# Two additions of an MLP convolution moved from VectorE to adding transfers on GpSimd's queue

## The chip, the cores and the metric

The kernel runs on one core of a Trainium2 chip. The core has a matrix engine (TensorE, PE in the profile; its weight loads are PEld), a vector engine (VectorE, DVE), an activation engine (ScalarE, ACT), a general engine (GpSimd, POOL) and a queue engine (SyncE, SP). Each works through its own instructions in order and waits on semaphores for the others. Transfers are issued from a queue of one of the engines and carried out by 16 DMA engines. The metric is the device time of one execution in microseconds, as a median of several.

## What is computed

An encoder trunk of two layers over 256 tokens of 1024 channels, in fp32. The first half of a layer is a token mixer (pooling and attention branches). The second half, which the change is about, is a gated MLP with a depthwise convolution of width 3 along the tokens:

```python
def _conv_ffn(xn, w_up, conv_w, conv_b, w_down):
    a, gval = jnp.split(xn @ w_up, 2, axis=-1)
    a = lax.conv_general_dilated(a, conv_w[:, None, :], window_strides=(1,),
                                 padding=((CONV_WIDTH // 2, CONV_WIDTH // 2),),
                                 dimension_numbers=('NWC', 'WIO', 'NWC'),
                                 feature_group_count=D_FF) + conv_b
    return (jax.nn.gelu(a) * gval) @ w_down
```

D_FF is 2816, that is 22 chunks of 128 channels. Token t of a channel needs the products of its own value, of the value before and of the value after, each with its own weight, and their sum.

## The kernel before

**Weight pieces.** TensorE multiplies numbers that are split into a high part in a shortened format and a rest, in three products (high by high, high by rest, rest by high). Every weight matrix is loaded from HBM in tiles `raw` (three buffers, loads on SP, L163), and each half of a tile, a *piece* of 128 x 1024, is split by a cast on ScalarE (`wh`, L242) and a subtraction on VectorE (`wl`, L244). There are five buffers for split pieces. `W.get()` takes the next piece for TensorE and splits the pieces ahead; in the stretches with an order written out by hand it opens the piece four ahead, whose buffer is that of the piece just used up. `open_next` returns the two steps of a split, and `run_between` puts waiting VectorE steps between them.

**Places.** The MLP is a row of *places*, one for each piece, with 12 matmuls of 512 columns each. `MLP_GROUPS` (L43) lists groups of four places: "a" are columns of the convolved branch, "g" of the gate branch, "b" the last two chunks of both, and "d" are rows of w_down: the product of the results with w_down accumulates in four PSUM banks. The group that is entered first has places 4 to 7; the loop at L1471 counts places from 8 on.

**Crossings.** An "a" or "g" group gives rows of tokens. At the first place of the next group, `cross` (L737) turns them on VectorE in blocks, writes 512 KB to DRAM from SP, and some places later SP reads them back with channels on the partitions (`zga`, `zg`, `zb`).

**Pairs.** The 22 chunks are taken in 11 pairs. For a pair, `steps_up(f)` gives five steps:

- `fetch_up` (ScalarE, L1397): from the crossed branch, for each of the two chunks, the product for the token before (`a0`), the middle one with bias (`y`), and that for the token after (`a2`), brought into the order of the tokens;
- `neighbours` (VectorE, L1409): two additions, of `a0` into `y` shifted by one token, and of `a2` into `y` shifted the other way;
- `activate` (ScalarE, L1414): the Gelu, in place on `y`;
- `gate` (VectorE, L1417): times the gate branch;
- `keep_up` (L1424): the split of the product into two parts, as TensorE needs it (copy on ScalarE, subtraction on VectorE).

`PAIR_PLACES` (L48) gives for each pair (p1, p3). Steps in `between` of a place run on VectorE between the cast and the rest of the piece opened there; steps in `behind` come behind the place's work, sorted by rank. Before the change: fetch behind p1, neighbours between at p1 + 1, activate behind p1 + 1, gate between at p3 and keep_up behind p3. Each list is in the engine's own order, so an engine that waits in one step holds everything behind it.

**The end of the MLP.** `residual_mm` (L615) multiplies with w_down. The last four rows of chunks (18 to 21) are held back and used together. When no pair step is left, the order by hand ends and the last pieces are run with the order that the scheduler makes (L1487 to L1493). The first layer goes over into the next layer's norm and value products, the second into the last norm and the stores.

Of the kernel before, what the change touches and what calls it, by code (L numbers as in the profile page):

```python
# [13 lines left out]
ALU = mybir.AluOpType  # L14
# [4 lines left out]
S = 256  # L19
# [21 lines left out]


MLP_GROUPS = (  # L43
    ("g", 0), ("a", 1), ("g", 1), ("d", 0), ("a", 2), ("g", 2), ("a", 3), ("g", 3), ("b", 20),
    ("a", 4), ("g", 4), ("d", 4), ("d", 8), ("d", 12), ("d", 16), ("d", 20),
)

PAIR_PLACES = (  # L48
    (11, 14), (14, 16), (19, 22), (23, 26), (31, 34), (35, 38), (40, 42), (44, 46), (51, 54), (56, 58), (53, 56),
)  # L50
HALVES = (slice(0, 512), slice(512, D))
SEGMENTS = (HALVES, (slice(0, 512), slice(512, 768), slice(768, D)))

# [226 lines left out]
def encoder(ctx, tc, x, w_in, w_pool, pool_scale, w_a, w_b, w_o, norm1, norm2, w_up, conv_w,  # L280
            conv_b, w_down, rel_bias, norm_f, onehot, edges, out):
    nc = tc.nc
# [28 lines left out]
    for l in range(DEPTH):  # L311
# [8 lines left out]
        for kind, n in GROUPS:  # L320
            c0 = {"u": 0, "q": C_Q, "k": C_K}[kind] + n * 512
            pieces = rows(w_in[l], 0, 4, c0, 512)
            if (kind, n) in POOLS:
                g, at = POOLS[kind, n]
# [445 lines left out]
    def begin_values_of_x():  # L770
# [32 lines left out]
        def square(t, n):  # L803
            cc = HALVES[n]
            junk = sm.tile([P, 512], F32, tag="p", bufs=3, name="junk")
            nc.scalar.activation(
                junk, h[:, t, cc], AF.Square, scale=D**-0.5, accum_out=ss[t][:, n : n + 1]
            )
            if n == 0:
                nc.gpsimd.tensor_scalar_add(ss[t][:, 3:4], ss[t][:, 0:1], EPS)  # L810
            else:
                nc.gpsimd.tensor_add(out=ss[t][:, 3:4], in0=ss[t][:, 3:4], in1=ss[t][:, 1:2])
                return nc.gpsimd.tensor_tensor(out=rs[t], in0=ss[t][:, 3:4], in1=mhalf, op=ALU.pow)
# [146 lines left out]
    for l in range(DEPTH):  # L960
# [274 lines left out]
        def keep_gated(n):  # L1235
# [4 lines left out]
            for t in range(2):  # L1240
                nc.vector.scalar_tensor_tensor(
                    out=gated["pa"][:, t, HALVES[n]], in0=th[t], scalar=1.0, in1=ps[t],
                    op0=ALU.add, op1=ALU.mult,
# [28 lines left out]
        with tc.manual_schedule():  # L1272
# [27 lines left out]
            first = None  # L1300
            for n, cc in enumerate(HALVES):
                ps = None
# [10 lines left out]
                y = big.tile([P, 2, 4, 4, 32], F32, tag=("q0", "k0")[n], name="turned")  # L1313
                z = big.tile([P, 2, 4, 4, 32], F32, tag=("q1", "v0")[n], name="merged")
                first = []
                for t in range(2):
                    nc.vector.scalar_tensor_tensor(
                        out=th[:, t], in0=th[:, t], scalar=1.0, in1=ps[t], op0=ALU.add, op1=ALU.mult
# [52 lines left out]
        def branch(kind, f, count=1):  # L1371

            n, c = divmod(f, 4)
            z, c = (z_of[kind, n], c) if n < NQ else (z_of["b", 4 * NQ], c + 2 * (kind == "g"))
            return z[:, :, c : c + count].rearrange("p (t a) c j -> p c t a j", t=2)
# [13 lines left out]
        def steps_up(f):  # L1389

            t = {}

            def row(j, c):
                k = j * NF + f + c
                return prm[:, l, k : k + 1]

            def fetch_up():  # L1397
                for name, tag in (("a0", "u"), ("y", "s"), ("a2", "us")):
                    t[name] = sm.tile([P, 2, S], F32, tag=tag, name=name)
                for c in range(2):  # L1400
                    a = branch("a", f + c)[:, 0]
                    for j, name in enumerate(("a0", "y", "a2")):
                        out = t[name][:, c].rearrange("p (a j t) -> p t a j", t=2, j=32)
                        if j == 1:
                            nc.scalar.activation(out, a, AF.Identity, bias=row(3, c), scale=row(1, c))
                        else:
                            nc.scalar.mul(out=out, in_=a, mul=row(j, c))  # L1407

            def neighbours():  # L1409
                y = t["y"]  # L1410
                nc.vector.tensor_add(out=y[:, :, 1:], in0=y[:, :, 1:], in1=t["a0"][:, :, : S - 1])
                nc.vector.tensor_add(out=y[:, :, : S - 1], in0=y[:, :, : S - 1], in1=t["a2"][:, :, 1:])

            def activate():  # L1414
                nc.scalar.activation(t["y"], t["y"], AF.Gelu_apprx_tanh)

            def gate():  # L1417
                g = t["g"] = sm.tile([P, 2, 2, P], F32, tag="p", bufs=3, name="g")
                nc.vector.tensor_mul(
                    out=g.rearrange("p c t (a j) -> p c t a j", j=32),  # L1420
                    in0=t["y"].rearrange("p c (a j t) -> p c t a j", t=2, j=32), in1=branch("g", f, 2),
                )

            def keep_up():  # L1424
                n = f % NH
                ah, al = (x[n >= HPG][:, n - HPG * (n >= HPG) :][:, 0:2] for x in (acth, actl))
                nc.scalar.copy(out=ah, in_=t["g"])
                nc.vector.tensor_sub(out=al, in0=t["g"], in1=ah.bitcast(F32))
                for c in range(2):
                    acts[f + c] = (ah[:, c], al[:, c])  # L1430

            return fetch_up, neighbours, activate, gate, keep_up

        between, behind = {}, {}
        for f, (p1, p3) in zip(range(0, NF, 2), PAIR_PLACES):
            fetch_up, neighbours, activate, gate, keep_up = steps_up(f)
            for at, p, rank, step in (
                (behind, p1, 2, fetch_up), (between, p1 + 1, 1, neighbours), (behind, p1 + 1, 1, activate),
                (between, p3, 0, gate), (behind, p3, 0, keep_up),
            ):  # L1440
                at.setdefault(p, []).append((rank, f, step))
# [82 lines left out]
```

## Time and profile before

| | us |
|---|---|
| median of 3 runs | 855.04 (854.87 to 856.85) |
| the profiled execution | 854.74 |
| its span, first to last instruction | 853.0 |
| TensorE busy in the span | 846.1 |
| VectorE busy | 606.0 |
| ScalarE busy | 501.1 |
| GpSimd busy | 34.8 |

The mean granted TensorE clock is 0.998. HBM gives 186.02 MB and takes 27.28 MB. The busy time is a sum over the span; the time that an engine did not work shows who waited only together with the waits. A matmul is recorded until its result has left the pipe, so one after the other they overlap. The MLP of the first layer lies at about 250 to 427 us of the span, that of the second at about 670 to 850.

### The profile page before, as it was taken

Reading aid. Unit: us, or ns where it says so; the run is one execution under the profiler, and the core shown is the slowest. Engines: PE = TensorE matmul, PEld = TensorE weight load, DVE = VectorE, ACT = ScalarE, POOL = GpSimd, SP = SyncE. Lnnn points to the kernel's source line nnn. Section 1 sums busy time; section 2 is a strip of 40 time slices with the busy share of each in tenths; the row PEclk is TensorE's granted clock in tenths of the full one; section 3 lists DMA queues with packets and bytes.
Section 4 is the critical chain, followed back from the end, with each engine's and each line's share of the span. In section 5 each row is a group of like instructions: output and inputs, shape, how many; then the busy total and the mean of one; then the engine's idle time right before and its main releaser. Section 6 shows DMA issues by size and latency. Waiting matters only on the chain.

```text
span 853.0 us, 10910 instructions
## 1 busy us (share of the span) xinstructions
PE 846.1 (99%) x3925; PEld 706.7 (83%) x3925; DVE 606.0 (71%) x794; ACT 501.1 (59%) x727; POOL 34.8 (4%) x96
## 2 busy tenths in 40 slices
PE   9999999999999999999999999999999999999997
PEld 7888888888888888888888888888888888888886
DVE  6958877767766776777755687868577767777674
ACT  7744566654543775758545454577454557566682
POOL 1710000000010000000000000000000100000000
PEclk9999999999999999999999999999999999999999
DMA  8698897796747979997726899768777489898931
GB/s 302 213 304 284 302 287 251 250 295 212 249 179 281 280 258 299 285 297 223 243 102 214 261 281 324 252 224 262 244 261 267 145 288 303 248 287 291 296 141 50
DMA packets 147966, 214.03 MB, mean 251 GB/s; under 512 B 7800, under 2 KB 69184, under 8 KB 147912
## 3 DMA queue, kind: packets, MB, share of 16 engines
q1 hardware_dynamic: 147480, 212.67, 76.6%
q8 instruction: 31, 0.51, 0.2%
q10 hardware_dynamic: 432, 0.66, 0.2%
q14 instruction: 23, 0.19, 0.1%
HBM read 186.02 MB, written 27.28 MB: 250 GB/s over the span
## 4 chain that ended last, share of the span: by engine, by line
PE 98%; DVE 1%; ACT 0%; POOL 0%; issue 0%; DVEq 0%; ACTq 0%; POOLq 0%
PE t_ps L694 64%; PE v_ps L694 6%; PE res_ps L611 6%; PE res_ps L612 6%; PE res_ps L613 6%; PE v_ps L940 3%; PE v_ps L839 1%; PE pool_ps L598 1%; PE o_ps L1223 1%; PE s_ps L1175 1%; PE s_ps L1170 1%; PE o_ps L1219 1%; PE xt_ps L525 1%; PE warm_ps L400 0%; PE xt_ps L790 0%; DVE h L505 0%
## 5 line engine op out<-in xcount | busy, mean ns | idle before, releaser
L244 DVE TENSOR_TENSOR wl<-raw,wh 128x1024 fp32r<-128x1024 f32 x274 | 331.7, 1220 | 157.5 <-ACT wh L242 156.4
L694 PE MATMUL t_ps<-wh,x 128*128 128x512 f32 x1408 | 439.2, 390 | 0.0
L242 ACT CAST wh<-raw 128x1024 fp32r<-128x1024 f32 x274 | 285.0, 1049 | 200.6 <-PE t_ps L694 132.0
L694 PEld LDWEIGHTS t_ps<-wh,x 128*128 128x128 f32 x1408 | 264.3, 188 | 55.0
L694 PE MATMUL t_ps<-wl,x 128*128 128x512 f32 x704 | 273.9, 389 | 0.0
L694 PEld LDWEIGHTS t_ps<-wl,x 128*128 128x128 f32 x704 | 132.2, 188 | 27.2
L613 PE MATMUL res_ps<-wh,actk 128*128 128x512 f32 (+1 forms) x184 | 69.8, 380 | 0.0
L611 PE MATMUL res_ps<-wh,actq 128*128 128x512 f32 (+1 forms) x184 | 69.8, 380 | 0.0
L612 PE MATMUL res_ps<-wl,actq 128*128 128x512 f32 (+1 forms) x184 | 69.7, 380 | 0.0
L694 PE MATMUL t_ps<-wh,po 128*128 128x512 f32 x128 | 41.4, 395 | 0.0
L612 PEld LDWEIGHTS res_ps<-wl,actq 128*128 128x128 f32 x184 | 34.6, 188 | 6.7
L613 PEld LDWEIGHTS res_ps<-wh,actk 128*128 128x128 f32 x184 | 34.6, 188 | 6.6
L611 PEld LDWEIGHTS res_ps<-wh,actq 128*128 128x128 f32 x184 | 34.6, 188 | 6.5
L1407 ACT ACTIVATE a<-zga,prm 128x256 f32<-128x256 f32 x80 | 39.0, 514 | 0.0
L490 POOL TENSOR_SCALAR ss<-ss 128x1 f32<-128x1 f32 x8 | 2.1, 266 | 771.9 <-ACT junk L483 771.9
L694 PEld LDWEIGHTS t_ps<-wh,po 128*128 128x128 f32 x128 | 24.1, 188 | 4.9
L611 PE MATMUL res_ps<-wh,m 128*128 128x512 f32 (+1 forms) x72 | 26.5, 368 | 0.0
L612 PE MATMUL res_ps<-wl,m 128*128 128x512 f32 (+1 forms) x72 | 26.3, 365 | 0.0
L744 DVE STREAM_TRANSPOSE crossing<-t_ps 128x512 f32<-128x512 f32 x40 | 26.1, 691 | 0.0
L613 PE MATMUL res_ps<-wh,m 128*128 128x512 f32 (+1 forms) x72 | 26.0, 366 | 0.0
L694 PE MATMUL v_ps<-wh,x 128*128 128x512 f32 x80 | 25.7, 392 | 0.0
L483 ACT ACTIVATE junk<-h 128x512 f32<-128x512 f32 (+1 forms) x19 | 10.5, 554 | 25.2 <-DVE h L505 25.0
(190 smaller groups left out, 923.6 us busy)
## 6 DMA issues: line engine op xcount, KB each, us to landing
raw<-in_w_in_dram SPq DMA_DIRECT2D x58, 1024.0 KB
raw<-in_w_up_dram SPq DMA_DIRECT2D x40, 1024.0 KB
raw<-in_w_down_dram SPq DMA_DIRECT2D x22, 1024.0 KB
crossing<-crossing SPq DMA_DIRECT2D x22, 512.0 KB
crossing<-way SPq DMA_DIRECT2D x16, 512.0 KB
raw<-in_w_a_dram SPq DMA_DIRECT2D x8, 1024.0 KB
raw<-in_w_o_dram SPq DMA_DIRECT2D x8, 1024.0 KB
zga<-crossing SPq DMA_DIRECT2D x40, 128.0 KB
```

Of the source, the lines that this page charges most:

```text
L242: inst = nc.scalar.copy(out=h, in_=src)
L244: inst = self.rests[i] = nc.vector.tensor_sub(out=l, in0=src, in1=h.bitcast(F32))
L483: nc.scalar.activation(junk[:, 0 : cc.stop - cc.start], h[:, t, cc], AF.Square, scale=D**-0.5, accum_out=ss[:, n : n + 1],)
L525: nc.tensor.transpose(pt[:, k, :], xn[:, c0 : c0 + P], ident)
L598: nc.tensor.matmul(out, w(k), x, start=(steps is first and k == 0), stop=(steps is last and k == nk - 1), skip_group_check=turns["rest"],)
L611: nc.tensor.matmul(ps, ah, wh, start=first, stop=False, skip_group_check=on)
L612: nc.tensor.matmul(ps, ah, wl, start=False, stop=False, skip_group_check=on)
L613: nc.tensor.matmul(ps, al, wh, start=False, stop=last, skip_group_check=on)
L694: nc.tensor.matmul(ps, x2[:, 2 * n + j, part, t, :], w[:, j, :], start=(n + m == 0), stop=(n == last and m == 5),)
L744: nc.vector.transpose(out=y[:, t].rearrange("p q c j -> p c q j"), in_=rows[t])
L940: nc.tensor.matmul(ps[t], a[:, k, t, :], w[:, j, :], start=(k + m == 0), stop=(k == KD - 1 and m == 2),)
L1407: nc.scalar.mul(out=out, in_=a, mul=row(j, c))
```

## The change

The two additions of `neighbours` become two transfers from SBUF to SBUF, issued on GpSimd's queue, that add what they read to their destination. Both write `y`, and their destinations overlap, so the second is issued after the first has landed. The step moves from between p1 + 1 to behind p1, after the fetch, and the Gelu from behind p1 + 1 to behind p1 + 3. p3 is p1 + 4 for every pair. The four w_down pieces of group ("d", 0) come after the branch group ("a", 2) and not before it.

```diff
 MLP_GROUPS = (
-    ("g", 0), ("a", 1), ("g", 1), ("d", 0), ("a", 2), ("g", 2), ("a", 3), ("g", 3), ("b", 20),
+    ("g", 0), ("a", 1), ("g", 1), ("a", 2), ("d", 0), ("g", 2), ("a", 3), ("g", 3), ("b", 20),
     ("a", 4), ("g", 4), ("d", 4), ("d", 8), ("d", 12), ("d", 16), ("d", 20),
 )
 
 PAIR_PLACES = (
-    (11, 14), (14, 16), (19, 22), (23, 26), (31, 34), (35, 38), (40, 42), (44, 46), (51, 54), (56, 58), (53, 56),
+    (11, 15), (14, 18), (19, 23), (23, 27), (31, 35), (35, 39), (40, 44), (44, 48), (51, 55), (56, 60),
+    (53, 57),
 )
...
             def neighbours():
                 y = t["y"]
-                nc.vector.tensor_add(out=y[:, :, 1:], in0=y[:, :, 1:], in1=t["a0"][:, :, : S - 1])
-                nc.vector.tensor_add(out=y[:, :, : S - 1], in0=y[:, :, : S - 1], in1=t["a2"][:, :, 1:])
+                for out, a in ((y[:, :, 1:], t["a0"][:, :, : S - 1]), (y[:, :, : S - 1], t["a2"][:, :, 1:])):
+                    nc.gpsimd.dma_start(out=out, in_=a, accum_op=ALU.add)
...
-                (behind, p1, 2, fetch_up), (between, p1 + 1, 1, neighbours), (behind, p1 + 1, 1, activate),
+                (behind, p1, 2, fetch_up), (behind, p1, 3, neighbours), (behind, p1 + 3, 1, activate),
                 (between, p3, 0, gate), (behind, p3, 0, keep_up),
```

## The prediction

> **What bounds the kernel now.** I read the page's busy line first, then the chain that ended last, then TensorE's own waits. The page (busy time of each engine, then shares of the chain by engine and by line):
>
> ```profile
> PE 846.1 (99%) x3925; PEld 706.7 (83%) x3925; DVE 606.0 (71%) x794; ACT 501.1 (59%) x727; POOL 34.8 (4%) x96
> ...
> PE 98%; DVE 1%; ACT 0%; POOL 0%; issue 0%; DVEq 0%; ACTq 0%; POOLq 0%
> PE t_ps L694 64%; PE v_ps L694 6%; PE res_ps L611 6%; PE res_ps L612 6%; PE res_ps L613 6%; PE v_ps L940 3%; PE v_ps L839 1%; PE pool_ps L598 1%; PE o_ps L1223 1%; PE s_ps L1175 1%; PE s_ps L1170 1%; PE o_ps L1219 1%; PE xt_ps L525 1%; PE warm_ps L400 0%; PE xt_ps L790 0%; DVE h L505 0%
> ```
>
> TensorE's waits, all of them (engine and line, what it waited for, us in total, times, longest):
>
> ```profile
> PE warm_ps L400 <- PEq L1506: 0.8, 1, 0.8
> ```
>
> The windows view over the first layer's MLP, in stretches of four places (us, then busy time of PE, PEld, DVE, ACT and POOL, granted clock, DMA share, GB/s):
>
> ```profile
> 268.34:279.23 10.89, 10.89 (x50) 9.02 (x49) 6.05 (x8) 5.37 (x8) 0.00 (x0) 1.00 0.95 345
> ...
> 322.77:333.65 10.88, 10.88 (x50) 9.01 (x49) 6.12 (x7) 5.49 (x8) 0.00 (x0) 1.00 1.04 282
> 333.65:344.54 10.89, 10.89 (x50) 9.02 (x49) 8.51 (x11) 7.78 (x14) 0.00 (x0) 1.00 1.04 312
> ...
> sum 174.14, PE 174.13 PEld 144.64 DVE 124.08 ACT 110.86 POOL 3.27; mean PE 10.88 PEld 9.04 DVE 7.76 ACT 6.93 POOL 0.20
> ```
>
> TensorE bounds: 98% of the chain is its own work, its only recorded wait is one of 0.8 us at the start, and in the MLP it is busy for 174.13 of 174.14 us at clock 1.00. VectorE and ScalarE run beside it. So whatever is taken from VectorE in the MLP buys nothing at the end; the question is only whether the new transfers make TensorE wait.
>
> **What goes.** The tile view of y (duration min/median/max in ns) has the two additions and the gate multiplication:
>
> ```profile
> L1411 DVE TENSOR_TENSOR y<-y,a x22: 646/691/693, 280.4 to 823.4; 128x510 f32<-128x510 f32 x22
> L1412 DVE TENSOR_TENSOR y<-y,a x22: 690/691/693, 281.1 to 824.2; 128x510 f32<-128x510 f32 x22
> ...
> L1419 DVE TENSOR_TENSOR g<-y,zg x20: 646/684/687, 285.6 to 825.9; 128x512 f32<-128x512 f32 x20
> ```
>
> 44 additions of 0.691 us are 30.4 us of VectorE, hidden beside TensorE: gain 0. Each gate, with its split, moves one or two places later (four in one case), also hidden so long as its result is not needed sooner. Four down pieces and one branch group change places: the same matmuls, casts, loads and crossings in another order. SP's two w_down loads go behind two of w_up and one crossing comes four places earlier, all with at least a group's time before their use: 0.
>
> **The cover the new transfers have.** The length of a place comes from the chain view (start, us, matmuls in a row), ScalarE's part of pair 4 from its timeline, and the costs of a weight piece from the page's groups (count, busy us, mean ns):
>
> ```profile
> 301.36 76.16 PE t_ps L694 x336
> ```
>
> ```profile
> 331.32 1.05 ACT L242 CAST wh<-raw 128x1024 fp32r<-128x1024 f32 x1 [1.62 <-PE t_ps L694]
> 332.27 0.53 ACT L1407 ACTIVATE a<-zga,prm 128x256 f32<-128x256 f32 x1
> ...
> 334.01 0.60 ACT L1405 ACTIVATE y<-zga,prm 128x256 f32<-128x256 f32 x1
> 334.51 0.51 ACT L1407 ACTIVATE a<-zga,prm 128x256 f32<-128x256 f32 x1
> 334.91 1.03 ACT L242 CAST wh<-raw 128x1024 fp32r<-128x1024 f32 x1
> 336.25 0.63 ACT L1415 ACTIVATE y<-y 128x512 f32<-128x512 f32 x1 [0.31 <-DVE y L1412]
> ...
> 340.43 0.62 ACT L1427 CAST actq<-g 128x512 fp32r<-128x512 f32 x1
> ```
>
> ```profile
> L244 DVE TENSOR_TENSOR wl<-raw,wh 128x1024 fp32r<-128x1024 f32 x274 | 331.7, 1220 | 157.5 <-ACT wh L242 156.4
> ...
> L242 ACT CAST wh<-raw 128x1024 fp32r<-128x1024 f32 x274 | 285.0, 1049 | 200.6 <-PE t_ps L694 132.0
> ```
>
> A place is 12 matmuls: 76.16/336 x 12 = 2.72 us. The 336 are places 20 to 47, so place 31 opens at 301.36 + 11 x 2.72 = 331.28, counted by matmul ends. The cast at 331.32 is of the piece for place 35; it waited for the buffer of place 30. Cast plus rest (1.05 + 1.22) end 2.3 us into the place, and TensorE takes the piece 10.5 us in (four places, less the 0.4 us that a matmul lies in the pipe). So ScalarE or VectorE may fall **8.2 us** behind before TensorE waits.
>
> The fetch begins 1.0 into place p1 and its second y ends at 334.61, 3.3 in. The Gelu now stands behind the cast of p1+3, which ends at 3 x 2.72 + 1.1 = 9.2. With a transfer of length L (issue to landing, the second issued when the first has landed), 2L has 9.2 - 3.3 = 5.9 us: **up to L = 2.95 nobody waits**. Behind a waiting Gelu stand ScalarE's casts and the next fetch, and VectorE's gate with the rests behind it; TensorE waits for those.
>
> Beyond that the pairs chain. With pairs four places apart, from fetch to next fetch: 2.3 to y, 2L, Gelu 0.6, one cast 1.0, split copy 0.6: 4.5 + 2L against 10.88, so a lag grows from L = 3.2 on. The gaps between fetches (3, 5, 4, 8, 4, 5, 4, 7 places) decide: at L = 4 the cycles are 11.0 for three places, 12.5 for four, and a further 1.0 for each place more; the lag peaks at 4.3, under 8.2, so TensorE still runs, and the gap of seven places brings it to nothing.
>
> The **end of each MLP** is tighter. Fetches are at places 51, 53 and 56 (pairs 8, 10, 9), GpSimd's queue runs in order, and the last fetch stands behind pair 10's Gelu. Six transfers run in series: y at 3.3, 4L, Gelu 0.6, fetch to y 2.3, 2L, Gelu 0.6, cast 1.0, rest 1.2 and the split's rest 0.7: 6L + 9.7 after place 51 opens. TensorE needs that pair's split at place 62, 11 x 2.72 - 0.4 = 29.5 after: **late by 6L - 19.8**, zero at L = 3.3.
>
> **L.** No trace row shows a transfer within SBUF, one that adds, or one from GpSimd's queue. The nearest are SP's. Its timeline (start, us of issuing) and ScalarE's wait on the smallest of them:
>
> ```profile
> 269.60 0.37 SPq L746 DMA_DIRECT2D crossing<-crossing  x1
> ...
> 274.67 1.81 SPq L753 DMA_DIRECT2D zg<-crossing  x4
> ...
> 378.40 0.38 SPq L746 DMA_DIRECT2D crossing<-crossing  x1
> ...
> 381.62 1.80 SPq L753 DMA_DIRECT2D zg<-crossing  x4
> ```
>
> ```profile
> 211.12 4.93 SPq L725 DMA_DIRECT2D merged<-turned  x8
> ```
>
> ```profile
> 217.68 0.62 ACT L732 CAST m<-merged 128x512 fp32r<-128x512 f32 x1 [0.32 <-DMA merged<-turned]
> ```
>
> A 512 KB write lands 274.67 - 269.97 = 4.7 or 381.62 - 378.78 = 2.8 us after issue; the last 64 KB read within 217.68 - 216.05 = 1.6. The addition has 128 x 510 x 4 B = 261 KB to read from the source, as much from its destination, and to write back. So L lies between 1.6 (it behaves like the smallest read) and 4.7 (like the slowest write). It reads 522 KB, about a crossing's size, beside the same loads, and GpSimd must issue it: I take the middle of the crossings and a little more, **L = 4.0**, an estimate. Then 6 x 4.0 - 19.8 = 4.2 us per layer, two layers **8.4 us**. GpSimd itself has nothing else to do there:
>
> ```profile
> POOL ss L490 <- ACT junk L483: 771.9, 8, 228.2
> ```
>
> The Trainium skill, "DMA: Bandwidth & Descriptors", section "Anatomy of one DMA — SWDGE (gpsimd) path", fits a transfer from GpSimd as about 2.0 us plus bytes over 436 GB/s: 2.6 us here, or 3.2 if the destination's read counts too, an estimate from that page. By it L would be under 3.3 and the sum 0; the 2.8 to 4.7 us of the crossings, twice the bytes under load, neither confirm nor refute it.
>
> **Load on the DMA engines.** The page's queue row gives packet time:
>
> ```profile
> q1 hardware_dynamic: 147480, 212.67, 76.6%
> ```
>
> A pair adds 2 x 261 KB written and up to 2 x 522 KB read; counted as 0.52 to 1.04 MB in 10.88 us that is 48 to 96 GB/s on top of the 282 to 312 above, against 345 in the densest stretch seen. The share reads 1.04 at 282 GB/s and 0.95 at 345, so it is no cap by itself. Nearly full engines are why I put L over the crossings' middle; for the weight loads I count 0 (lower end 0; upper end in the third rival).
>
> **The sum.** The profiled execution took 854.74 us: 853.0 of span, 1.74 around it. 854.74 + 8.4 = 863.1; the median 855.04 lies 0.3 above that execution, so 863.4, told as 863. At L = 4.7 the lag reaches 8.2 in the dense stretches (3.7 us of waits) and enters the end chain at 6.1: 3.7 + 6.1 + 8.4 = 18.2 per layer, 891 in all. At L up to 3.3: 855.
>
> **Rivals.**
> First, the **cover holds**: L at or under 3.3. For it: the 2.8 us of a 512 KB write, and 8.2 us of pieces ready ahead. Against it: two reads for each write, and engines nearly full. It decides at L = 3.3 and gives 855, no change: the rival on the other side.
> Second, **GpSimd is held up or the adding is slow**, L of 4.5 or more. The mechanism would be that VectorE's instructions (mean 1.22 us a rest, and 8.51 of 10.89 us busy) hold up the writing of the transfer's descriptors, about one rest for each: L = 5.2. The chain then gives 10.7 us of waits in the dense stretches and 11.4 + 7.1 at the end, 29.2 per layer, 913. Against it: the trace shows no such hold, as GpSimd has no work there. The Trainium skill, "SBUF — State Buffer", section "SBUF: two separate sides", describes this lock for two-port modes of VectorE alone; the MLP's two-input subtractions at 0.84 elements per ns look like none, and by that rule this rival falls.
> Third, **weight loads come late**: 312 + 96 = 408 GB/s against 345 would stretch a dense four places by 18%, 2.0 us. Eight such pairs are 16 us a layer, less 8.2 of cover: 8 a layer, 871. Against it: half of that traffic may never count, and gaps lie between.
> Fourth, **faster**: VectorE's relief shortens a wait. Nothing in the MLP is there to shorten; the 6.9 us in which TensorE is not busy lie outside it. At most 2 or 3 of them: 852.
>
> **How the numbers follow.** Forecast (L from 3.3 to 4.5) 0.40; cover holds 0.33; held up or slow adding 0.19; late loads 0.05; faster 0.03. About 0.3% (2.6 us) is what a measurement of this kernel can tell from no change. Of the forecast's case some 0.04 lies within it (L under 3.5). So slower 0.36 + 0.19 + 0.05 = 0.60, same 0.33 + 0.04 = 0.37, faster 0.03. The range runs from 854 (cover holds) to 900, where L is 4.9; outside lie the faster case and about two thirds of the slow one, 0.16. The likeliest case alone spans 855 to 883.
>
> **What would show it.** Right: in the changed profile TensorE's waits in the MLP sit at place 62 of each layer (about 416 and 836 us), behind the split of L1428 or the rests L244; the Gelu on ScalarE waits for a DMA into y, about 2L - 5.9 for a pair that stands alone, so some 2 us, and over 4 for pairs 10 and 9; VectorE is 30 us less busy; GpSimd's queue shows 44 transfers with starts about 4 us apart. Wrong: if starts of one pair's two transfers are under 3.3 us apart there are no waits and 855; over 4.5, TensorE waits all through the MLP. If TensorE waits while those starts are short, casts that wait for raw would point to late loads, and my account of the cover would be at fault.

## The result and the profile after

The changed kernel took 985.44 us (median of 4; 981.93 to 985.88) against 854.96 beside it: a ratio of **1.151, 95% interval 1.148 to 1.154**, slower by 130.5 us. The forecast was 863, its range 854 to 900. The direction was right and the size far off.

The page of the changed kernel (span; busy time of each engine; granted clock in 40 slices; the chain that ended last by engine):

```profile
span 984.1 us, 11004 instructions
...
PE 894.1 (91%) x3925; PEld 729.9 (74%) x3925; DVE 576.5 (59%) x750; ACT 495.2 (50%) x727; POOL 87.8 (9%) x140
...
PEclk9999999999998799879699999999999978987888
...
PE 58%; DMA 27%; ACT 8%; issue 3%; DVE 2%; SPq 0%; POOL 0%; ACTq 0%; POOLq 0%; DVEq 0%
```

TensorE's waits in it (engine and line, what it waited for, us in total, times, longest):

```profile
PE t_ps L697 <- ACT wh L245: 31.3, 9, 6.3
PE res_ps L614 <- ACT wh L245: 24.2, 5, 7.1
PE res_ps L614 <- ACT actq L1430: 18.0, 4, 6.2
PE t_ps L697 <- DVE wl L247: 6.1, 10, 0.8
PE res_ps L615 <- DVE wl L247: 2.9, 6, 0.8
```

TensorE's 98% of the chain have become 58%, and transfers have 27% where they had none. The additions alone hold 24% of it (`DMA y<-a`). VectorE is 29.5 us less busy, as it should be. TensorE waits 82.5 us in these five rows, 73.5 of them for casts of ScalarE (L245 for weight pieces, L1430 for the split of a pair), and is busy 48.0 us more with the same 3925 matmuls: together 130.5, the whole loss. The granted clock has 6 to 8 tenths in some slices of the MLP.

Why ScalarE's casts come late stands in its own waits (engine and line, what it waited for, us in total, times, longest; the first and the last row are the Gelus, of which one in each layer has its wait ahead of a table load) and in the timelines of ScalarE and GpSimd over the first two pairs (start, us; in brackets the idle time before it):

```profile
ACT y L1418 <- DMA y<-a: 178.5, 20, 15.8
...
ACT wh L245 <- DMA raw<-in_w_up_dram: 24.6, 6, 5.7
...
ACT L1418 <- DMA y<-a: 20.1, 2, 11.5
```

```profile
297.66 1.28 ACT L1418 ACT_TABLE_LOAD   x1 [11.55 <-DMA y<-a]
298.95 0.63 ACT L1418 ACTIVATE y<-y 128x512 f32<-128x512 f32 x1
...
315.40 0.63 ACT L1418 ACTIVATE y<-y 128x512 f32<-128x512 f32 x1 [9.89 <-DMA y<-a]
```

```profile
280.50 1.39 POOL L1415 DMA_DIRECT2D y<-a  x1 [31.64 <-DVE crossing L747]
292.98 1.21 POOL L1415 DMA_DIRECT2D y<-a  x1 [11.10 <-DMA y<-a]
302.08 1.20 POOL L1415 DMA_DIRECT2D y<-a  x1 [7.89 <-ACT y L1408]
306.39 1.19 POOL L1415 DMA_DIRECT2D y<-a  x1 [3.12 <-DVE crossing L747]
320.98 1.19 POOL L1415 DMA_DIRECT2D y<-a  x1 [13.40 <-ACT y L1408]
```

The 22 Gelus wait 198.6 us for the two additions, 9.0 each. The first pair's additions begin at 280.50 and 292.98 and its Gelu at 298.95, the second's at 302.08 and 306.39 and its Gelu at 315.40. From issue to landing, over all 44 (tile view of y):

```profile
DMA to landing us min/median/max: 3.6/6.0/11.9
```

The issuing itself takes a steady 1.2 us. What lies beside five of the transfers (window, us, busy time of PE, PEld, DVE, ACT, POOL, granted clock, DMA share, GB/s; each window from issue to landing, the transfer's own bytes included):

```profile
280.50:292.43 11.93, 11.93 (x54) 9.86 (x54) 3.68 (x3) 3.11 (x4) 1.38 (x1) 1.00 1.02 289
302.08:305.85 3.77, 2.23 (x4) 1.45 (x5) 2.72 (x4) 3.43 (x5) 1.20 (x1) 0.55 0.48 69
306.39:315.36 8.97, 8.53 (x32) 6.53 (x30) 2.03 (x2) 0.00 (x0) 1.19 (x1) 0.84 0.95 245
425.99:429.76 3.77, 3.77 (x12) 2.92 (x12) 2.71 (x3) 2.93 (x4) 1.20 (x1) 0.64 0.68 86
430.30:434.57 4.27, 4.27 (x20) 3.54 (x19) 1.47 (x3) 0.00 (x0) 1.20 (x1) 1.00 1.08 340
```

Where the DMA engines moved 69 and 86 GB/s an addition took 3.8 us; at 245 and 289 GB/s it took 9 and 12, but at 340 GB/s only 4.3. Over all 44 it is the same: the 12 with less than 120 GB/s took 3.6 to 4.7 us, the 30 with 208 or more took 4.3 to 11.9, and the two between took 7.2 and 7.6. So no addition was long without traffic, and traffic alone doesn't say how long. That suggested the theory: **the length of a transfer hangs on what else is under way**, and a pair, from its first addition to its Gelu, takes 14 us where its additions were to take 8.

### The profile page after: what moved, and what is told of

The parts are those of the page before. It is cut to its first block, busy times and chain, and to the rows that moved or that the text cites. A ratio compares the mean times of both kernels' runs of the same rounds, so it can differ in the third digit from the quotient of the medians.

```text
span 984.1 us, 11004 instructions
## 1 busy us (share of the span) xinstructions
PE 894.1 (91%) x3925; PEld 729.9 (74%) x3925; DVE 576.5 (59%) x750; ACT 495.2 (50%) x727; POOL 87.8 (9%) x140
## 4 chain that ended last, share of the span: by engine, by line
PE 58%; DMA 27%; ACT 8%; issue 3%; DVE 2%; SPq 0%; POOL 0%; ACTq 0%; POOLq 0%; DVEq 0%
PE t_ps L697 38%; DMA y<-a 24%; PE v_ps L697 6%; ACT wh L245 4%; PE res_ps L614 2%; PE res_ps L615 2%; PE v_ps L943 2%; ACT a L1410 2%; PE res_ps L616 2%; DMA zg<-crossing 2%; ACT y L1408 2%; PE pool_ps L601 1%; PE v_ps L842 1%; DMA raw<-in_w_up_dram 1%; PE o_ps L1226 1%
## 5 line engine op out<-in xcount | busy, mean ns | idle before, releaser
L697 PE MATMUL t_ps<-wh,x 128*128 128x512 f32 x1408 | 455.3, 401 | 31.3 <-ACT wh L245 31.3
L245 ACT CAST wh<-raw 128x1024 fp32r<-128x1024 f32 x274 | 280.8, 1046 | 154.4 <-PE t_ps L697 101.6
L697 PEld LDWEIGHTS t_ps<-wh,x 128*128 128x128 f32 x1408 | 273.0, 194 | 92.8 <-ACT wh L245 35.6
L697 PE MATMUL t_ps<-wl,x 128*128 128x512 f32 x704 | 282.9, 402 | 6.1 <-DVE wl L247 6.1
L614 PE MATMUL res_ps<-wh,actq 128*128 128x512 f32 (+1 forms) x184 | 79.0, 429 | 42.2 <-ACT wh L245 24.2
L1422 DVE TENSOR_TENSOR g<-y,zg 128x512 f32<-128x512 f32 x20 | 13.8, 692 | 160.8 <-ACT y L1418 160.8
L1418 ACT ACTIVATE y<-y 128x512 f32<-128x512 f32 x22 | 13.9, 630 | 178.5 <-DMA y<-a 178.5
L1415 POOL DMA_DIRECT2D y<-a x44 | 53.0, 1224 | 394.1 <-ACT y L1408 230.4
L615 PE MATMUL res_ps<-wl,actq 128*128 128x512 f32 (+1 forms) x184 | 78.4, 426 | 3.0 <-DVE wl L247 2.9
L616 PE MATMUL res_ps<-wh,actk 128*128 128x512 f32 (+1 forms) x184 | 75.1, 412 | 0.1
L614 PE MATMUL res_ps<-wh,m 128*128 128x512 f32 (+1 forms) x72 | 26.5, 368 | 0.0
```

Of the source, the lines that this page charges most:

```text
L245: inst = nc.scalar.copy(out=h, in_=src)
L614: nc.tensor.matmul(ps, ah, wh, start=first, stop=False, skip_group_check=on)
L615: nc.tensor.matmul(ps, ah, wl, start=False, stop=False, skip_group_check=on)
L616: nc.tensor.matmul(ps, al, wh, start=False, stop=last, skip_group_check=on)
L697: nc.tensor.matmul(ps, x2[:, 2 * n + j, part, t, :], w[:, j, :], start=(n + m == 0), stop=(n == last and m == 5),)
L1415: nc.gpsimd.dma_start(out=out, in_=a, accum_op=ALU.add)
```

## The experiments

**Parts of the change alone.** First, the new order of groups, gates and Gelus, with the additions back on VectorE (label order_only):

```diff
-                for out, a in ((y[:, :, 1:], t["a0"][:, :, : S - 1]), (y[:, :, : S - 1], t["a2"][:, :, 1:])):
-                    nc.gpsimd.dma_start(out=out, in_=a, accum_op=ALU.add)
+                nc.vector.tensor_add(out=y[:, :, 1:], in0=y[:, :, 1:], in1=t["a0"][:, :, : S - 1])
+                nc.vector.tensor_add(out=y[:, :, : S - 1], in0=y[:, :, : S - 1], in1=t["a2"][:, :, 1:])
...
-                (behind, p1, 2, fetch_up), (behind, p1, 3, neighbours), (behind, p1 + 3, 1, activate),
+                (behind, p1, 2, fetch_up), (between, p1 + 1, 1, neighbours), (behind, p1 + 3, 1, activate),
```

> The changed order of groups and places, Gelu three places behind the fetch, but both additions on VectorE again. If the transfers alone are the loss: 855 us, within 1.5. If the order of the groups or the later gates cost something: up to 985, the part of it that is theirs.

Measured: 854.61 us, ratio 0.9992 (0.9982 to 1.0001). The order costs nothing, so all of the loss is the transfers'.

Second, the additions on GpSimd, but as two instructions in place of two transfers (gpsimd_adds):

```diff
-                    nc.gpsimd.dma_start(out=out, in_=a, accum_op=ALU.add)
+                nc.gpsimd.tensor_add(out=y[:, :, 1:], in0=y[:, :, 1:], in1=t["a0"][:, :, : S - 1])
+                nc.gpsimd.tensor_add(out=y[:, :, : S - 1], in0=y[:, :, : S - 1], in1=t["a2"][:, :, 1:])
```

> The changed order with the two additions as instructions of GpSimd itself, no transfers. If only the length of the pair of additions counts, and an addition takes under 2.9 us there: 855 within 1.5. If GpSimd and VectorE hold each other up so that splits come late: more, 860 to 900.

Measured: 854.72, ratio 0.9997 (0.9988 to 1.0007). The instructions took 1.29 and 2.09 us (medians). VectorE is 16.3 us less busy, TensorE waits for nothing but the 0.8 us at the start, and nothing is gained: VectorE's relief is worth nothing here.

**The transfer by itself.** Both layers are left out; eight of each kind run one after the other, first with nothing beside them, then beside a stream of 1 MB weight loads on SP. In the first try (alone) the loads were meant to start behind the quiet part.

```diff
+        for r in raw:
+            nc.vector.tensor_copy(r[:, 0, 0:1], y[:, 0, 0:1])
+        for n in range(120):
...
+            nc.sync.dma_start(out=raw[n % 3], in_=src)
```

> Only transfers between two tiles, eight of a kind one after the other: first with nothing else moving, then beside a stream of 1 MB loads on SP's queue. The layers are left out. Theory (loads): an addition takes long because SP's loads and crossings are served ahead of it; then a quiet one lands about 3.6 to 4.6 us after issue, as the quickest in the changed kernel, and one beside the stream 8 to 12 us or more, whether it adds or copies. Rival (adding): the second read and the addition are slow by themselves; then the quiet additions take 6 us or more, the copies clearly less, and the stream changes little. Rival (rows): every short row takes a turn with a packet of the loads; then rows of 2 KB for 1 KB halve what the stream adds. Rival (held): VectorE's work holds up GpSimd's issuing; VectorE does nothing here, so beside the stream all stays near 4 us.

The byte read by that copy is one that the transfers don't write, so the loads began at once, and at times SP's queue stood still in between: the phases are mixed, and the run decides nothing by itself. The next two put three loads ahead of each transfer and wait on a byte that it does write (apart and apart_gpsimd). In apart the loads paused again, from about 190 to 232 us, so that the long rows lost them after two and GpSimd's copies had none; apart_gpsimd leaves out ScalarE's queue and has the kinds in the other order, and its loads ran throughout.

```diff
-            nc.vector.tensor_copy(r[:, 0, 0:1], y[:, 0, 0:1])
+            nc.vector.tensor_copy(r[:, 0, 0:1], y[:, 0, 1:2])
...
+        for step in (beside_add, beside_add_long, beside_copy, beside_copy_act):
+            for _ in range(N):
+                for _ in range(3):
+                    load(n)
+                    n += 1
+                step()
```

> The transfers between two tiles again, now eight of each kind one after the other first with nothing else moving, and then with three loads of 1 MB put in for each. Theory (loads): a quiet addition lands about 4 us after issue (the last one of the earlier run took 4.0 to the next start), an addition beside loads about 8, copies in the same relation, 2.8 and 5 or more. Rival (adding): quiet and loaded alike, 6 us or more. Rival (rows): the long rows beside loads take half of what the short ones take over their quiet time.

> Transfers between two tiles from GpSimd's queue alone, quiet and beside loads, this time with copies beside loads too. If what the loads add grows with the bytes that a transfer reads: copies about 2.8 quiet and 5 beside loads, additions 4.1 and 8.2, long rows 3.6 and 7.1. If it grows with the count of rows: copies and additions gain the same 4.1, long rows 2.

GpSimd's timeline in apart, additions with nothing beside them and then beside the loads:

```profile
8.87 1.20 POOL L121 DMA_DIRECT2D y<-a  x1 [5.25 <-DMA y<-a]
12.98 1.19 POOL L121 DMA_DIRECT2D y<-a  x1 [2.91 <-DMA y<-a]
17.05 1.19 POOL L121 DMA_DIRECT2D y<-a  x1 [2.87 <-DMA y<-a]
```

```profile
128.08 1.19 POOL L133 DMA_DIRECT2D y<-a  x1 [7.22 <-DMA y<-a]
136.37 1.19 POOL L133 DMA_DIRECT2D y<-a  x1 [7.09 <-DMA y<-a]
144.54 1.19 POOL L133 DMA_DIRECT2D y<-a  x1 [6.98 <-DMA y<-a]
```

From start to start, in us (beside loads, GpSimd's kinds are from apart_gpsimd, where the DMA engines moved 359 to 382 GB/s; ScalarE's is from apart, where they moved 251 in that phase):

| kind (GpSimd's queue unless said) | quiet | beside loads |
|---|---|---|
| addition, rows of 255 elements, as in the change | 4.07 | 8.25 |
| addition in rows of 511 | 3.57 | 7.0 to 7.4 |
| plain copy | 2.82 | 6.26 |
| plain copy, ScalarE's queue | 2.50 | 5.44 |

By itself an addition takes about the 4.0 us that the prediction took (4.07 from start to start, 3.8 of it from issue to landing). Beside loads it takes twice that, and VectorE has no work in these phases. The load adds 3 to 4 us to every kind, neither in proportion to the bytes read nor to the rows: both expectations on that missed. How the queues share the engines is not settled by it.

**Other transfers in the kernel.** plain_copies copies over `y` and leaves the sum out. long_rows adds in rows of 511 elements, which puts one wrong product in at the join of two chunks:

```diff
-                    nc.gpsimd.dma_start(out=out, in_=a, accum_op=ALU.add)
+                    nc.gpsimd.dma_start(out=out, in_=a)
```

```diff
-                for out, a in ((y[:, :, 1:], t["a0"][:, :, : S - 1]), (y[:, :, : S - 1], t["a2"][:, :, 1:])):
+                y, a0, a2 = (t[name].rearrange("p c s -> p (c s)") for name in ("y", "a0", "a2"))
+                for out, a in ((y[:, 1:], a0[:, : 2 * S - 1]), (y[:, : 2 * S - 1], a2[:, 1:])):
```

> The changed kernel with the two transfers copying over y and not adding to it; the convolution's sum is left out. Theory (loads): a copy waits beside the loads as an addition does, two of them still 10 us or more for a pair, 920 to 985 us. Rival (adding): a transfer of about 3.5 us, where the cover of 8.2 us suffices, 855 to 865.

> The changed kernel with each addition as one row of 511 values a partition and not two of 255, so half as many rows for the same bytes; one wrong product is added at the join of a pair. Theory (loads): the transfer still lands when the loads ahead of it are served, 950 to 985 us. Rival (rows): half the turns, a transfer of 4 to 4.5 us, 865 to 880.

Measured: copies 923.99, ratio 1.080 (1.077 to 1.083), 5.3 us to landing in the median; long rows 953.96, ratio 1.115 (1.111 to 1.120), 5.5 us. Without the adding about half of the loss is gone, with long rows a quarter; a plain copy would still lose 69 us.

**The load taken away.** In the MLP weight tiles are not loaded but the one before is used again: every second one where it has the same shape (half_loads), or all but the first of each run of one shape (no_loads, where 10 of the 70 transfers that load w_up and w_down remain). In half_loads a crossing's read that is held back until a load is issued waits for the next load where that one is left out; no_loads has no such delay. no_writes leaves the loads and leaves out the crossings' writes, no_loads_writes leaves out both.

```diff
+            last = self.n_loaded - 1
+            if self.n_loaded in self.again and self.loads[last][1:] == (shape, tag):
+                self.raw[self.n_loaded] = self.raw[last]
+                self.n_loaded += 1
...
+        W.again.update(range(begun_at + 1, len(W.loads)))
...
+        if W.by_hand and W.last_d is not None:
+            d = W.last_d
```

> The changed kernel, but in the MLP every second weight tile isn't loaded and the one before it is used again, so that half of the weights are left out and the DMA engines have half the loads; crossings stay. Theory (loads): transfers come down toward their quiet 4.07, some 5 each, 880 to 920 us. Rival (a transfer in this place is long for another cause): 975 to 985.

> The changed kernel, but in the MLP only the first weight tile is loaded and all the others of its shape reuse it; the crossings to DRAM and back stay, so what it computes is not the reference's. Theory (bytes that other queues have under way lengthen the adding transfers): those that fall beside no crossing take 3.6 to 4.1 us, those beside a crossing's 512 KB write stay at 8 to 10, the median to landing falls to about 4 and the time to 880 to 925. Rival (the work of the engines on SBUF, not the other transfers, lengthens them): the median stays at 4.7 us or more and the time at 945 or more, as with half of the loads.

> The changed kernel with all weight loads, but in the stretches ordered by hand only the first crossing of each is written to DRAM; the reads back stay, of that first block. Theory that the loads and the writes of the crossings both count, by bytes: the transfers beside loads stay at 7 to 9 us, the median to landing at 5 to 6, and the time at 940 to 970. Rival (the crossings' writes alone make the long transfers): the median falls to about 4 and the time under 900.

> As no_loads, and in the stretches ordered by hand only the first crossing of each is written to DRAM; the reads back stay, of that first block. What is left beside the adding transfers are those reads of 512 KB a group. Theory: the DMA engines are nearly empty, all transfers take 3.6 to 4.1 us, and the chain of the prediction at L = 4.1 gives 863 to 870, with TensorE's waits only at the end of each MLP, some 4 to 5 us each, as with GpSimd held for 8 us a pair. Rival (SBUF traffic of the engines): transfers of 6 us or more in the dense stretches and over 920.

Issue to landing, by the tile view of y, in half_loads, no_loads and no_writes in this order:

```profile
DMA to landing us min/median/max: 3.6/4.7/11.0
```

```profile
DMA to landing us min/median/max: 3.6/3.8/11.2
```

```profile
DMA to landing us min/median/max: 3.7/5.8/12.0
```

| | us | ratio |
|---|---|---|
| changed kernel | 985.44 | 1.151 (1.148 to 1.154) |
| no_writes | 970.93 | 1.134 (1.127 to 1.142) |
| half_loads | 948.62 | 1.110 (1.102 to 1.118) |
| no_loads | 908.88 | 1.062 (1.059 to 1.065) |
| no_loads_writes | 905.73 | 1.058 (1.055 to 1.062) |

Half of the loads gone gives back 37 us, nearly all of them 77: **the weight loads are what lengthens the additions** from 3.8 to 6.0 us in the median. The crossings' writes count for 3 us without the loads and 15 with them. half_loads missed its expectation of 880 to 920 and looked like evidence against the loads; beside no_loads it is simply half of the effect. The longest transfers are left in every run; in no_loads the first of them (from 281.07 on, 10.0 us) runs beside a crossing and one of the loads that remain.

no_loads_writes missed: 863 to 870 was expected, and the median to landing is 3.8 us as the theory says, yet 50 us of loss are left. The next part tells why.

**The wait alone.** GpSimd does the two additions as instructions, with idle instructions between them, and no transfer is there at all: 6 of them (gpsimd_8) or 13 (gpsimd_14).

```diff
+                nc.gpsimd.tensor_add(out=y[:, :, 1:], in0=y[:, :, 1:], in1=t["a0"][:, :, : S - 1])
+                for _ in range(13):
+                    nc.gpsimd.tensor_tensor(out=idle_r, in0=mhalf, in1=mhalf, op=ALU.pow)
+                nc.gpsimd.tensor_add(out=y[:, :, : S - 1], in0=y[:, :, : S - 1], in1=t["a2"][:, :, 1:])
```

> No transfers: both additions on GpSimd with six small powers between them that serve only to pass time, so that a pair takes about 8 us, as two transfers of the length that I forecast (4.0). By the chain as I worked it out: 863, within 6. If waiting is cheaper than that: 855. If a wait costs more than the chain counts (a slower clock after it): 870 or more.

> The same with thirteen powers, so that a pair takes some 13 to 14 us, about as long as the two transfers took, with nothing added to the DMA engines' work. If the wait alone makes the loss: by the chain 970 to 985. If the transfers' traffic makes weight loads and crossings late and that is the loss: under 900.

Measured: 868.45, ratio 1.016 (1.013 to 1.019), and 954.9, ratio 1.117 (1.113 to 1.121). TensorE's waits in gpsimd_8, the MLP's own in the first line:

```profile
PE res_ps L615 <- ACT actq L1433: 8.5, 2, 4.3
PE xt_ps L794 <- DMA h<-in_x_dram: 1.0, 1, 1.0
PE warm_ps L404 <- PEq L1512: 0.8, 1, 0.8
```

GpSimd's timeline over the first pair of gpsimd_14 (the fetch of the next pair ends at 295.5):

```profile
280.23 1.30 POOL L1415 TENSOR_TENSOR y<-y,a 128x510 f32<-128x510 f32 x1 [31.39 <-ACT y L1409]
281.48 10.05 POOL L1417 TENSOR_TENSOR idle_r<-mhalf 128x1 f32<-128x1 f32 x13
291.50 1.09 POOL L1418 TENSOR_TENSOR y<-y,a 128x510 f32<-128x510 f32 x1
295.53 1.30 POOL L1415 TENSOR_TENSOR y<-y,a 128x510 f32<-128x510 f32 x1 [2.95 <-ACT y L1409]
```

At 8 us a pair the kernel does what the prediction's sum says: one wait of 4.2 to 4.3 us at the end of each MLP, at 421.74 and 847.95 us and for the split of a pair. At 12.2 us it loses 100 us without a byte more on the DMA engines. (The pair came out shorter than the 13 to 14 us aimed at, and the time with it.)

Now ten of the runs can be put on one line. Call p the time from the start of a pair's first addition to the start of its Gelu, as a mean over the 22 pairs of each trace. By the prediction's own rows TensorE needs 51 places of 2.72 us, 138.7 us, from place 11 to 62, and 11 pairs in series need 11 x (4.5 + p). This is a coarser sum than the prediction's, which has the first wait at the end of an MLP. The difference, for two layers, stands beside the measured loss. In the runs with transfers p holds much of what was lost, so there the line is bookkeeping; in the gpsimd runs p was set from outside.

| | p, us | 2 x (11 x (4.5 + p) - 138.7) | loss measured |
|---|---|---|---|
| gpsimd_adds | 5.66 | -54 (the pairs keep up) | -0.2 |
| gpsimd_8 | 8.03 | -2 (the pairs just keep up) | 13.5 |
| no_loads_writes | 10.01 | 42 | 49.4 |
| no_loads | 10.25 | 47 | 52.5 |
| plain_copies | 11.03 | 64 | 69.0 |
| half_loads | 12.02 | 86 | 93.7 |
| gpsimd_14 | 12.20 | 90 | 100.0 |
| long_rows | 12.43 | 95 | 99.0 |
| no_writes | 13.19 | 112 | 114.6 |
| changed kernel | 13.79 | 125 | 130.5 |

From gpsimd_8 to gpsimd_14, without any transfer, 4.2 us more of p cost 86.5 us, 21 for each; from no_loads_writes to the changed kernel 3.8 us cost 81.1, again 21. So in these runs the loss is nearly all the pace of this chain: above a knee at p = 138.7/11 - 4.5 = 8.1 us **each microsecond of a pair costs about 22 us**. The 3 to 10 us that the losses lie above the line from p = 10 on fit waits at the end of an MLP as in gpsimd_8, but that was not separated. It also explains no_loads_writes: its p is 10.0 and not 8.1. In it, loads and reads that remain stretch the first pair of each layer to 19.9 and 17.8 us, and most others take 8 to 9.5.

**Two attempts at relief.** one_transfer leaves one addition on VectorE; late_gelu gives the transfers one place more:

```diff
+            def other():
+                y = t["y"]
+                nc.vector.tensor_add(out=y[:, :, : S - 1], in0=y[:, :, : S - 1], in1=t["a2"][:, :, 1:])
...
+                (behind, p1, 2, fetch_up), (behind, p1, 3, neighbours), (between, p1 + 3, 1, other), (behind, p1 + 3, 1, activate),
```

```diff
-                (behind, p1, 2, fetch_up), (behind, p1, 3, neighbours), (behind, p1 + 3, 1, activate),
-                (between, p3, 0, gate), (behind, p3, 0, keep_up),
+                (behind, p1, 2, fetch_up), (behind, p1, 3, neighbours), (behind, p1 + 4, 1, activate),
+                (between, p3 + 1, 0, gate), (behind, p3 + 1, 0, keep_up),
```

> The changed kernel with only the first addition as a transfer and the second on VectorE in the place of the Gelu. If the cover of the chain as I worked it out holds: one transfer of 6.5 to 7.2 us and an addition of 0.7 stand in 5.9 us and a lag of 8.2, so 855 to 862. If the traffic of the transfers on the DMA engines is what costs (half of it is left): about 920.

> The changed kernel with Gelu, gate and split one place later for every pair. The chain as I worked it out takes one cast out of each turn and 14 us a layer at the transfers' length of 6.5 to 7: about 957, within 10. If the DMA engines' throughput bounds and not the chain: no change, 985.

one_transfer took 885.57, ratio 1.036 (1.034 to 1.038): a miss for the 855 to 862 of the theory. Its transfers take 7.5 us in the median and up to 13.8. They are the first additions of the pairs, and in the changed kernel the first ones by themselves take 7.7 in the median, so that leaving the second ones out has not shortened them. Its p is 9.0 in the mean, for which the line gives 19 of the 30.6 us lost; the rest is not explained. TensorE's largest wait is then for VectorE's rests:

```profile
PE t_ps L697 <- DVE wl L247: 9.8, 8, 3.4
```

late_gelu took 937.39, ratio 1.096 (1.094 to 1.098). It gives back 48 us where 28 were expected, with transfers no shorter (median 6.6), so it is the waiting and not the transfers' throughput that costs. One thing that the expectation did not count is in the edit: the Gelus of the pairs fetched at places 11 and 53 move from 14 and 56 to 15 and 57, and so behind the fetches at 14 and 56. In the first layer two Gelus then follow each other at 303.40 and 308.75 with no fetch between them, so these pairs overlap and are no longer in series, and the line above doesn't hold for this run. How much of the 20 us this gives was not measured. Nothing that was run is faster than the kernel before: the nearest, order_only, can't be told from it.

## Why the prediction was right or wrong

**What bounds: right.** TensorE bounded, and nothing taken from VectorE bought time: gpsimd_adds 854.72, order_only 854.61. The zeros for the order and the later gates hold as well. The zero for the weight loads was not tested by itself: ScalarE's casts wait 24.6 us for loads of w_up in the changed kernel, but 25.6 in gpsimd_14 and 34.3 in gpsimd_8, where there is no transfer to delay them.

**The chain and the end of the MLP: right.** The knee was put at a transfer of 3.2 to 3.3 us in the densest stretches and the end of the MLP, and the late end at 6L - 19.8 = 4.2 us a layer for L = 4.0. gpsimd_8, at that pace, shows 4.3 and 4.2, behind the split and near the places that the prediction named. The time was 868 where the sum said 863: TensorE is busy 850.7 us there against 846.1, 4.6 us that the sum did not have.

**The length L: wrong, and this made most of the miss.** The step is "I take the middle of the crossings and a little more, L = 4.0", with 1.6 to 4.7 as its ends, and behind it "Nearly full engines are why I put L over the crossings' middle". 4.07 us is what an addition takes with nothing beside it. Beside a stream of loads it takes 8.25, and in the kernel, from issue to landing, 6.5 us in the mean and up to 11.9. By the prediction's own slope (891 at L = 4.7, 913 at 5.2) 6.5 gives about 970, an estimate; the other 15 us are not separated. That L = 4.0 meets the quiet figure is luck: it was taken from crossings beside loads. The crossings gave no bound: they were another kind of transfer, from another queue. And the prediction itself quoted one of 4.7 and one of 2.8 us, which it read as a range. The windows of just these two in the kernel before (columns as above, their own bytes included) were a hint that the load decides, with 412 GB/s beside the slow one and 252 beside the quick one:

```profile
269.97:274.67 4.70, 4.70 (x22) 3.89 (x21) 2.36 (x2) 2.48 (x3) 0.00 (x0) 1.00 1.05 412
378.78:381.62 2.84, 2.84 (x14) 2.37 (x13) 1.34 (x2) 1.05 (x1) 0.00 (x0) 1.00 0.81 252
```

**The range.** The prediction saw how steep its chain was: 891 at L = 4.7, 900 at 4.9, 913 at 5.2. With that slope an upper end of 4.7, taken from rows of another kind, should not have closed the range at 900.

**The rival of 0.19 got the size of the effect nearest, and half of its reason.** It was "GpSimd is held up or the adding is slow". The adding is slower than a copy, 4.07 against 2.82 us with nothing beside them, and a copy in the kernel loses 69 us and not 130.5. But the mechanism that gave its price, VectorE holding up the writing of descriptors, is not what happened: issuing took a steady 1.2 us in the changed kernel, and the additions took 8.25 us where VectorE had no work. The Trainium skill, "SBUF — State Buffer", section "SBUF: two separate sides", has a lock that keeps GpSimd from writing descriptors while VectorE runs in a two-port mode; the steady issuing beside two-input subtractions agrees with that. Late weight loads are not the cause either: gpsimd_14 loses 100 us with the loads as before. The load on the DMA engines did matter, but in the other direction: the loads made the additions late.

**The page's fit.** The 2.0 us plus bytes over 436 GB/s of the Trainium skill ("DMA: Bandwidth & Descriptors", section "Anatomy of one DMA — SWDGE (gpsimd) path") gave an estimate of 2.6 us. A quiet copy from start to start takes 2.82, near it; a quiet addition 4.07, and beside loads they take 6.26 and 8.25. The measurement decides: here the fit holds for a plain copy with nothing beside it.

**What would show it.** "Starts over 4.5 us apart: TensorE waits all through the MLP" came true, with starts 7.2 us apart in the mean. What was left out of that list is the spread: 4.1 to 12.5 in one kernel.

## What to carry to other kernels

Price a transfer beside the traffic that it will run in, by a row of its own kind or a kernel that measures just that; a quiet price was right here and worthless. Two transfers that must follow each other, in an engine's order by hand, are a chain with a pace: compare that pace with the pace of the engine that bounds before anything else, because beyond the knee every microsecond is paid once for each turn (here about 22 times). Where the estimate lies at the knee, the range must reach as far up as the slope takes the worst price.

## What the hardware showed

A wait costs more than its length. TensorE's timeline in the changed kernel, after a wait of 4.53 us (start, us of one or two matmuls) and six us later:

```profile
303.15 0.79 PE L697 MATMUL t_ps<-wh,x 128*128 128x512 f32 x1 [4.53 <-ACT wh L245]
...
307.56 1.05 PE L697 MATMUL t_ps<-wh,x 128*128 128x512 f32 x2
308.42 0.63 PE L697 MATMUL t_ps<-wl,x 128*128 128x512 f32 x1
308.85 0.59 PE L697 MATMUL t_ps<-wh,x 128*128 128x512 f32 x1
309.27 0.40 PE L614 MATMUL res_ps<-wh,actq 128*128 128x512 f32 x1
309.51 0.39 PE L615 MATMUL res_ps<-wl,actq 128*128 128x512 f32 x1
```

Until 309.27 the matmuls come 0.43 us apart and then 0.23. The window from 303.15 to 309.27 has a granted clock of 0.50 (the figure before the DMA share): half speed for 6.1 us after the wait.

```profile
303.15:309.27 6.12, 5.65 (x12) 4.09 (x13) 5.27 (x6) 2.36 (x3) 1.32 (x2) 0.50 0.66 141
```

The Trainium skill, "TensorE: Matmul & The Clock Gate", section "Part 1: The HAM clock gate", has this as a gate that halves the clock after an idle window of about 3.4 us and opens again after as long a busy one; the trace agrees in kind, with a longer slow stretch here. The 48.0 us more of busy TensorE come with it (the mean granted clock is 0.943 against 0.998), though in a kernel whose pairs set the pace part of that would otherwise have been waiting.

An addition of 128 x 510 elements from GpSimd's queue occupies GpSimd for 1.2 us to issue, one in rows of 511 elements 0.86, and a copy 0.72 (apart). The two additions as instructions took GpSimd 1.29 and 2.09 us in gpsimd_adds and hid completely beside TensorE.
